# A hybrid decoder layer in float32 on one core: wide triples between bursts of chunk products, four array tiles at once, and 56 instead of 48 fill triples per group

## The chip, the core and the metric

The kernel runs on one core of one Trainium2 chip. The metric is device microseconds (us) of one execution; the figure compared is the median of several runs. The engines have short names here: PE is TensorE (matrix products; PEld its weight loads), DVE is VectorE, ACT is ScalarE, POOL is GpSimd, and SP is SyncE, which issues most DMAs.

## What is computed

One layer of a causal decoder, sequence 1024, width 1024, batch 1, all in float32. Cut to what matters:

```python
h = rms_norm(x, norm_mix_pre); z = h @ w_in          # ONE input projection for all branches and gates
z_pool, z_q, z_rwkv, z_gate = split(z)
y_pool = pool_branch(z_pool, ...) @ w_proj_pool
y_mem  = mem_attention(z_q, mem_n, w_mem_kv) @ w_proj_mem
zr = z_rwkv + (token_shift(z_rwkv) - z_rwkv) * mu_shift
r, k, v, dw, da, dg = split(zr)
def step(state, (rt, wt, kt, vt, an, bn)):           # 16 heads of 64, 1024 steps
    sa = state @ an
    state = state * wt + sa (x) bn + vt (x) kt       # (x): outer product
    yt = state @ rt
y_rwkv = (group_norm(y) + bonus) * g @ w_proj_rwkv
x = x + rms_norm((gates[0]*y_pool + gates[1]*y_rwkv + gates[2]*y_mem) @ w_o)
x = x + rms_norm((gelu(u_gate) * u_val) @ w_ffn_down)   # u = causal_dwconv(rms_norm(x) @ w_ffn_up)
```

The recurrence is done in 16 chunks of 64 steps: for each head and chunk a few 64x64 products, the inverse of a unit triangular 64x64 matrix, and then a short serial chain from chunk to chunk.

## The kernel before

**Wide triples.** A float32 product is made of three products of rounded parts: for a weight tile and 512 columns, `mm3` issues three matmuls of 128x128 by 128x512 (lines 180, 181, 182). I call these three a wide triple. Their weights come by DMA (`wraw`), are rounded on ACT (`whi`, line 132) and the rest is made on POOL (`wlo`, line 139).

**Preparations.** `rwkv_group(g, kv)` runs four times (g = 0 to 3), for four heads each, in two halves i = 0, 1 of 128 partitions (two heads, "lo" and "up"). In a group, in this order of the code:

- `lengths` (tile `phd`), then the decay and in-context rates (tile `psu`, lines 502 and 503), on ACT the sigmoids and exponentials, on DVE the scans and the factors `AR`, `BK`; the projection of r (`in_block(8 + p, ...)`, 48 wide matmuls per half) lies in between. The last reader of the scratch tile `tHV` is line 552.
- The centred values (tile `pv`, lines 577 and 578): 64 matmuls of 64x64 per group; each row of 64 partitions writes the other half of a PSUM tile. ACT copies them into `HV` (lines 579, 580), which has the memory of `tHV`.
- The chunk products (line 601): for each half i four bursts of 8 matmuls into two PSUM banks each; the four banks of `product_bank` (two of `pss`, one of `psk`, one of `psc`) go round, so a burst needs the banks of the burst before last. ACT copies two parts out of a burst (lines 605, 608) and DVE masks four (lines 606, 607, 609, 610).
- After the bursts of i = 0: the bonus (tile `pbo`, line 562, multiplied on DVE in line 563), and for each half the transposes of `BK` (tile `pt`, line 630, copied by ACT in line 631).
- The projection of the next group's k and v (`group_kv`, 192 wide matmuls), and on DVE the inverse of 32x32 blocks by 31 steps (lines 651 to 655), which ends with eight copies (line 664). Then PE joins the blocks: tile `pz` (line 672), copies by ACT and DVE, tile `pw` (line 680).

**Fill.** Blocks of the input projection that nobody needs soon (pool, query and gates: 32 blocks, 512 triples) are issued by `fill_to(n)`, which advances them until n triples are out. Before, a group asks for 48 more of them at the end of its solve; group 3 goes on to 256.

**Chain.** `chain` then walks over the 16 chunks with three visits each (tiles `pr`; `py` and `pu`; `ph` and `py`; all line 772). Before each visit it calls `fill_to(fills(visit))`: 262 at the first, then 279 rising to 400 at the last. Every two chunks use one set of loads (`ring`, `pair`, `hv`, `bk`, `rb`), sent ahead on SP's queue one per visit; the loads for chunks 2b and 2b+1 are sent during the two chunks before. Meanwhile the finished chunks are normed (tile `pvar`) and stored, and the fill's weights come on ACT's queue.

**Order.** A list scheduler orders the built instructions of each engine. `later(i, j)` is a dependence for that order alone; the engines wait for data and for buffers only.

Of the kernel before, what the change touches and what calls it, by code (L numbers as in the profile page):

```python
# [9 lines left out]
F32 = mybir.dt.float32  # L10
# [7 lines left out]
P = 128  # L18
# [3 lines left out]
C = 64  # L22
# [6 lines left out]
NF = 22  # L29
HK = NF // 2  # L30
LAST = HK - 4

PV = {}
_o = 0
# [10 lines left out]
def trunk_kernel(ctx: ExitStack, tc: tile.TileContext, xT, memT, pvec, w_in, w_kv, w_upd, w_upg,  # L45
                 w_pool, w_ppool, w_pmem, w_prwkv, w_o, w_fup, w_fdn, out):
    nc = tc.nc
    V, A, G, PE, SP = nc.vector, nc.scalar, nc.gpsimd, nc.tensor, nc.sync
# [53 lines left out]
    for lo in (0, 64):  # L102
        s = slice(lo, lo + 64)
# [371 lines left out]
    def rwkv_group(g, kv):  # L475
# [11 lines left out]
        def lengths():  # L487
            for i in range(2):
                for s, ps in square_sums(kv[i][:, 0], col("k_k", 2 * g + i), tHV[:, i, 1], sp[:, i]):
                    rstd(tHV[:, i, 1, s], ps, 1)  # L490

        if g:
            lengths()
            table(SIGMOID)
        for i in range(2):
            p = 2 * g + i
            uh, ul = load_up2(w_upd[p])
            for t0, _ in HALVES:
                s = slice(t0, t0 + 512)
                for e, l, dst, b in ((0, ld, tBN[i][:, 0, s], "w0"), (1, la, tHV[:, i, 0, s], "a0")):  # L500
                    ps = psg.tile([P, 512], F32, name="psu", tag="g0")
                    PE.matmul(ps, uh[:, e], l[:, s], start=True, stop=False)
                    PE.matmul(ps, ul[:, e], l[:, s], start=False, stop=True)
                    act(dst, ps, AF.Sigmoid, bias=col(b, p))
        table(LN_EXP)
        if g == 0:
            lengths()
        AR = rw.tile([P, 2, 3, T], F32, name="AR", tag="AR")
        vs = []
        turn = [0]  # L510

# [58 lines left out]
        NT = rw.tile([P, 2, NCH, C], F32, name="NT", tag="NT")  # L570
        HV = rw.tile([P, 2, NCH, C], F32, name="HV", tag="HV")
        for i in range(2):
            for c0 in (0, 8):
                ps = pss.tile([P, 8, C], F32, name="pv", tag="s")
                for c in range(8):
                    tsl = slice((c0 + c) * C, (c0 + c + 1) * C)
                    PE.matmul(ps[64:128, c], vs[i][0:64, tsl], cent[0:64], start=True, stop=True)
                    PE.matmul(ps[0:64, c], vs[i][64:128, tsl], cent[64:128], start=True, stop=True)
                A.copy(HV[64:128, i, c0:c0 + 8], ps[64:128])
                A.copy(HV[0:64, i, c0:c0 + 8], ps[0:64])  # L580
            spill(d_hv, (g, i), HV[:, i])


# [5 lines left out]
        for i in range(2):  # L589
            us = slice(NCH * i, NCH * i + NCH)  # L590
            for c0 in range(0, NCH, 4):
                def bc(m, q):
                    return m[q].unsqueeze(1).broadcast_to([64, 4, C])
                cs = slice(c0, c0 + 4)
                lo, up = slice(0, 64), slice(64, 128)
                ps = [product_bank("ps1"), product_bank("ps2")]
                m = None
                for c in range(4):
                    t = slice((c0 + c) * C, (c0 + c + 1) * C)
                    for e, rows in ((1, up), (0, lo)):  # L600
                        m, was = PE.matmul(ps[e][:, c], BK[i][rows, c0 + c], AR[rows, i, e:e + 2, t],
                                           start=True, stop=True), m
                        if was is not None:
                            later(m, was.ins)
                A.copy(RB[i][:, 0, cs], ps[0][:, :, 1])
                V.tensor_tensor(NT[lo, i, cs], ps[0][lo, :, 0], bc(mstrict, lo), op=ALU.mult)
                V.tensor_tensor(c3(AR[up, i, 0])[:, cs], ps[0][up, :, 0], bc(mstrict, up), op=ALU.mult)
                A.copy(RB[i][:, 1, cs], ps[1][:, :, 0])
                V.tensor_tensor(NT[up, i, cs], ps[1][up, :, 1], bc(mstrict, up), op=ALU.mult)
                V.tensor_tensor(c3(AR[lo, i, 2])[:, cs], ps[1][lo, :, 1], bc(mstrict, lo), op=ALU.mult)  # L610
            for e in range(2):
                V.tensor_tensor(RB[i][:, e], RB[i][:, e], mincl.unsqueeze(1).broadcast_to([P, NCH, C]),
                                op=ALU.mult)
# [13 lines left out]
            for c0 in range(0, NCH, 4):  # L627
                ps = pss.tile([P, 4, P], F32, name="pt", tag="s")
                for c in range(4):
                    PE.transpose(ps[:, c], BK[i][:, c0 + c], ident)  # L630
                A.copy(BKN[i][:, c0:c0 + 4], ps)
            SP.dma_start(d_bk[:, :, g, i].rearrange("c p u s -> p c (u s)"),
                         BKN[i].rearrange("p (c u) s -> p c (u s)", u=2))

            if i == 0:
                tb0 = rw.tile([P, 2, 32, 32], F32, name="tb0", tag=tagB[0])
            for q, (qs, bs) in enumerate(quads):
                if i == 0 or q < 2:
                    A.copy(tb0[qs, 1, us], NTu[qs, us, bs])
                else:  # L640
                    V.tensor_copy(tb0[qs, 1, us], NTu[qs, us, bs])
# [13 lines left out]
            V.tensor_tensor(S[:, s + 1:, 0:m], S[:, s + 1:, 0:m], tm, op=ALU.add)  # L655
        V.transpose(S11.rearrange("p u s -> p s u"), S.rearrange("p t s -> p s t"))
        V.transpose(X.rearrange("p u t -> p t u"), S)
        fill_to(48 * (g + 1))
        if g == 3:
            w_queue[0] = A  # L660
            fill_to(256, solve)
        for us in (slice(0, NCH), slice(NCH, 2 * NCH)):
            for q, (qs, bs) in enumerate(quads):
                place = V.tensor_copy(NTu[qs, us, bs], X[qs, us]).ins
        Z = tmp
        ends = [(slice(e, e + 32), slice(e + 32, e + 64)) for e in (0, 64)]
        for u0 in (0, 16):
            us = slice(u0, u0 + 16)
            ps = pss.tile([P, 16, 32], F32, name="pz", tag="s")
            for u in range(16):  # L670
                for q0, q1 in ends:
                    m = PE.matmul(ps[q1, u], NTu[q0, u0 + u, 32:64], S11[q0, u0 + u], start=True, stop=True)
                    if u0 == u == 0:
                        later(m, place)
            A.copy(Z[32:64, us], ps[32:64])
            V.tensor_copy(Z[96:128, us], ps[96:128])
            ps = pss.tile([P, 16, 32], F32, name="pw", tag="s")
            for u in range(16):
                for q0, q1 in ends:
                    PE.matmul(ps[q0, u], Z[q1, u0 + u], NTu[q1, u0 + u, 32:64], start=True, stop=True)  # L680
            for q0, q1 in ends:
                A.copy(NTu[q0, us, 32:64], ps[q0])


        for i in range(2):
# [161 lines left out]

    fill = [(j, spilled(d_zp[j])) for j in range(4)] + [(4 + j, spilled(d_zq[j])) for j in range(4)]
    fill += [(34 + j, spilled(d_zg[j], col("gate_b", j))) for j in range(24)]
    filled = []  # L850

    def fill_steps(j, evac, behind):

        ws = load_w(w_in[j], KC, c=1)
        for t0, _ in HALVES:
            ps = psg.tile([P, 512], F32, name="psg", tag="g1")
            rhs = hrhs(t0)
            for k in range(KC):
                m = mm3(ps, ws[k], rhs(k), k == 0, k == KC - 1)
                if k == 0 and behind is not None:  # L860
                    later(m, behind)
                filled.append(last_mm[0])
                if k == KC - 1:
                    evac(t0, ps)
                yield
# [3 lines left out]
    def fill_to(n, behind=None):  # L869

        while len(filled) < n:
            if next(current[0], 0) == 0:
                current[0] = fill_steps(*fill.pop(0), behind)
        return filled[n - 1]

    first_kv = start()
    for lo in (0, 64):
        s = slice(lo, lo + 64)
# [2 lines left out]
    hi_on_act[0] = True  # L881
    for g in range(4):
        kv = rwkv_group(g, kv)
    chain(lambda v: 279 + 121 * (v - 1) // 46 if v else 262)
    covered = fill_to(416)
    w_queue[0] = SP
    spare[0] = None
# [964 lines left out]
```

## Time and profile before

| | us |
|---|---|
| runs shown | 1952.37, 1947.69, 1952.64 (median 1952.37) |
| the profiled execution | 1947.9 |
| its span, first to last instruction | 1946.2 |
| first group's start to first `pr` of the chain | about 62 to 666 of the span |
| chain | 666 to 862 |
| attention, merge, feed-forward | 862 to the end |

In the profile, a row of the timeline has the start, the time from it to the end of the last of the xN merged instructions, engine, line, operation, tiles and form; in brackets stands the idle time of the engine before it and what ended that. A float32 matmul of a narrow kind is recorded as two instructions, so 8 of line 601 in the program are 16 records. A row of windows has the stretch, its length, the busy time and number of each engine's instructions, the granted PE clock as a share, the busy share of the 16 DMA engines and the GB/s.

### The profile page before, as it was taken

The page shows a single profiled execution, that of the slowest core. Times are in us where ns is not written, and L with a number is a line of the kernel's source. Part 1 is how long each engine was busy: PE and PEld are TensorE (multiplying, and loading weights), DVE is VectorE, ACT ScalarE, POOL GpSimd, SP SyncE. Part 2 cuts the span into 40 slices and gives each one's busy share as a digit, 9 for nine tenths or more (in the row PEclk, how much of TensorE's full clock was granted, in tenths as well). Part 3 has the DMA queues.
Part 4 walks back from the last instruction along what each step waited for, and adds up shares of the span by engine and source line. Part 5 has one row for each costly group of instructions (what it writes and reads, how often), then busy time and mean ns, then how long its engine had stood idle before and what let it go on. Part 6 is the DMA issues. An engine that isn't in the chain of part 4 may idle for free.

```text
span 1946.2 us, 33744 instructions
## 1 busy us (share of the span) xinstructions
PE 1886.9 (97%) x12204; PEld 1522.7 (78%) x12204; DVE 1356.7 (70%) x2022; ACT 1046.1 (54%) x2158; POOL 784.1 (40%) x867
## 2 busy tenths in 40 slices
PE   8999999999999999999999999999999999999997
PEld 6767777777777887778788888878788888888886
DVE  8677577677677345556964444679698888877798
ACT  7685385475474245455664344546554545454544
POOL 4422222222222211111323455556599889822441
PEclk9999999999999999999999999999999999999999
DMA  5326326335349669965336444653322222289775
GB/s 163 130 72 186 99 76 184 93 95 168 95 122 310 191 191 297 312 196 190 102 112 231 124 137 130 208 161 121 110 81 87 78 88 88 86 250 223 168 184 146
DMA packets 269639, 296.26 MB, mean 152 GB/s; under 512 B 18336, under 2 KB 219168, under 8 KB 266400
## 3 DMA queue, kind: packets, MB, share of 16 engines
q1 hardware_dynamic: 248480, 271.56, 44.8%
q0 software_dynamic: 11856, 14.16, 4.5%
q10 hardware_dynamic: 9136, 8.39, 1.4%
q8 instruction: 96, 1.57, 0.3%
q14 instruction: 71, 0.58, 0.1%
HBM read 207.00 MB, written 87.03 MB: 151 GB/s over the span
## 4 chain that ended last, share of the span: by engine, by line
PE 62%; DVE 5%; DMA 4%; issue 2%; ACT 2%; POOL 1%; ACTq 0%; POOLq 0%; DVEq 0%; SPq 0%
PE psg L180 10%; PE psg L182 10%; PE psg L181 10%; PE psf L182 6%; PE psf L180 6%; PE psf L181 6%; PE psd L181 2%; PE psd L182 2%; PE psd L180 2%; PE py L772 2%; PE pr L772 1%; DMA g<-d_zg 1%; PE ph L772 1%; PE pvar L716 1%; PE pu L772 1%
## 5 line engine op out<-in xcount | busy, mean ns | idle before, releaser
L139 POOL TENSOR_TENSOR wlo<-wraw,whi 128x256 fp32r<-128x256 f32 x464 | 403.0, 881 | 829.0 <-ACT whi L132 753.6
L180 PE MATMUL psg<-hh,whi 128*128 128x512 f32 x928 | 377.7, 407 | 12.4 <-ACT whi L132 9.0
L182 PE MATMUL psg<-hh,wlo 128*128 128x512 f32 x928 | 367.6, 397 | 1.8 <-POOL wlo L139 1.5
L181 PE MATMUL psg<-hl,whi 128*128 128x512 f32 x928 | 368.1, 397 | 0.7 <-DVE hl L266 0.6
L132 ACT CAST whi<-wraw 128x256 fp32r<-128x256 f32 x472 | 181.5, 403 | 246.8 <-PE psg L181 98.9
L180 PEld LDWEIGHTS psg<-hh,whi 128*128 128x128 f32 x928 | 174.8, 188 | 57.4 <-ACT whi L132 13.0
L182 PEld LDWEIGHTS psg<-hh,wlo 128*128 128x128 f32 x928 | 174.8, 188 | 44.1 <-POOL wlo L139 6.1
L181 PEld LDWEIGHTS psg<-hl,whi 128*128 128x128 f32 x928 | 175.0, 189 | 39.8 <-issue 4.3
L1178 POOL TENSOR_TENSOR wt<-a,wt 128x256 fp32r<-128x256 f32 x136 | 156.3, 1173 | 35.4 <-ACT wt L1177 35.2
L180 PE MATMUL psd<-f,u 128*128 128x512 f32 x292 | 113.3, 391 | 1.1 <-ACT f L1590 1.1
L181 PE MATMUL psd<-f,u 128*128 128x512 f32 x292 | 113.8, 390 | 0.5 <-DVE f L1594 0.5
L182 PE MATMUL psd<-f,u 128*128 128x512 f32 x292 | 113.6, 389 | 0.0
L182 PE MATMUL psf<-h2h,wt 128*128 128x512 f32 x272 | 105.9, 390 | 0.2 <-POOL wt L1178 0.2
L180 PE MATMUL psf<-h2h,wt 128*128 128x512 f32 x272 | 105.9, 389 | 0.1
L181 PE MATMUL psf<-h2l,wt 128*128 128x512 f32 x272 | 105.8, 389 | 0.0
L1192 DVE SCALAR_TENSOR_TENSOR d<-z,pv,d 128x1023 f32<-128x1023 f32 x68 | 101.1, 1491 | 2.2
L1178 POOL TENSOR_TENSOR wt<-s,wt 128x256 fp32r<-128x256 f32 x68 | 79.9, 1195 | 3.3 <-ACT wt L1177 2.0
L180 PE MATMUL psf<-t,wt 128*128 128x512 f32 x204 | 79.4, 389 | 0.0
L181 PE MATMUL psf<-t,wt 128*128 128x512 f32 x204 | 79.4, 389 | 0.0
L182 PE MATMUL psf<-t,wt 128*128 128x512 f32 x204 | 79.4, 389 | 0.0
L1190 ACT ACTIVATE d<-z,pv 128x1024 f32<-128x1024 f32 x34 | 42.4, 1248 | 65.8 <-DVE z L1272 50.1
L1177 ACT CAST wt<-a 128x256 fp32r<-128x256 f32 x136 | 50.7, 405 | 40.8 <-POOL wt L1178 28.1
(430 smaller groups left out, 4507.3 us busy)
## 6 DMA issues: line engine op xcount, KB each, us to landing
wraw<-in_w_in SPq DMA_DIRECT2D x176, 128.0 KB, 2.5
a<-in_w_fup SPq DMA_DIRECT2D x128, 128.0 KB, 2.4
d_ar<-AR SPq DMA_DIRECT2D x24, 512.0 KB, 4.2
d_zg<-st SPq DMA_DIRECT2D x48, 256.0 KB, 3.4
ring<-d_ar SPq DMA_DIRECT2D x8, 1536.0 KB, 10.8
wraw<-in_w_fup SPq DMA_DIRECT2D x80, 128.0 KB, 2.6
fraw<-d_f SPq DMA_DIRECT2D x33, 256.0 KB, 4.3
d_rb<-RB SPq DMA_DIRECT2D x16, 512.0 KB, 5.4
```

The source lines that it names most:

```text
L132: i = A.copy(hi, src)
L139: (V if lo_on_dve[0] else G).tensor_tensor(lo, src, hi.bitcast(F32), op=ALU.subtract)
L180: first = PE.matmul(ps, wh, xh, start=start, stop=False)
L181: PE.matmul(ps, wh, xl, start=False, stop=False)
L182: last_mm[0] = PE.matmul(ps, wl, xh, start=False, stop=stop).ins
L716: m = PE.matmul(ps, bones, q, start=True, stop=True)
L772: m = PE.matmul(out_, l, r, **kw)
L1177: A.copy(w[0][:, us], src[u])
L1178: low = eng.tensor_tensor(w[1][:, us], src[u], w[0][:, us].bitcast(F32), op=ALU.subtract)
L1190: A.activation(d, z, AF.Identity, scale=col("cw2", j), bias=col("cb", j))
L1192: V.scalar_tensor_tensor(d[:, n:], z[:, :T - n], col(cw, j), d[:, n:], op0=ALU.mult, op1=ALU.add)
```

## The change

It has five parts. (1) Between two bursts of chunk products stand two wide triples of the fill. (2) `pv`, `pz` and `pw` are issued so that four array tiles (two row groups by two column groups) follow each other; all copies of `pz` precede all of `pw`. (3) A group asks for 56 triples instead of 48, group 3 goes to 288 instead of 256, and the chain starts from there: 294 at its first visit, then 311 rising to 400. (4) At the head of groups 1 to 3 two lots of six triples are asked for behind fixed places, and one triple in group 0. (5) Two half tiles of `pv` (i = 1) use the banks `psk` and `psc` instead of `pss`.

```diff
+GROUP = 56
+TAKEN = 4 * GROUP + 64
...
+        cover, burst = [GROUP * g - 12 if g else 0], [None]
+
+        def covered(n, behind=None):
+            cover[0] += n
+            fence[0] = behind
+            wide = fill_to(cover[0])
+            fence[0] = None
+            return wide
+
+        if g:
+            covered(6, placed[0])
+            covered(6, raised[2])
+        else:
+            covered(1)
...
-            for c0 in (0, 8):
-                ps = pss.tile([P, 8, C], F32, name="pv", tag="s")
-                for c in range(8):
-                    tsl = slice((c0 + c) * C, (c0 + c + 1) * C)
-                    PE.matmul(ps[64:128, c], vs[i][0:64, tsl], cent[0:64], start=True, stop=True)
-                    PE.matmul(ps[0:64, c], vs[i][64:128, tsl], cent[64:128], start=True, stop=True)
+            ps = [pool.tile([P, 8, C], F32, name="pv", tag=tag)
+                  for pool, tag in (((psk, "k"), (psc, "c")) if i else ((pss, "s"), (pss, "s")))]
+            m = None
+            for c in range(8):
+                for n in (1, 0):
+                    t = slice((8 * n + c) * C, (8 * n + c + 1) * C)
+                    for rows, at_ in ((lo, lo if n else up), (up, up if n else lo)):
+                        m, was = PE.matmul(ps[n][at_, c], vs[i][rows, t], cent[rows], start=True, stop=True), m
+                        later(m, was.ins if was is not None else raised[-1])
...
                 ps = [product_bank("ps1"), product_bank("ps2")]
-                m = None
+                after = covered(2, burst[0]) if c0 else None
...
-        fill_to(48 * (g + 1))
+        fill_to(GROUP * (g + 1) - (12 if g < 3 else 0))
         if g == 3:
             w_queue[0] = A
-            fill_to(256, solve)
+            fill_to(TAKEN, solve)
...
-        for u0 in (0, 16):
-            us = slice(u0, u0 + 16)
-            ps = pss.tile([P, 16, 32], F32, name="pz", tag="s")
+        us = slice(0, 16), slice(16, 32)
+        ps = pss.tile([P, 16, 32], F32, name="pz", tag="s")
+        for u in range(16):
+            for h in range(2):
+                for ends_ in ends:
+                    m = PE.matmul(ps[ends_[1 - h], u], NTu[ends_[0], 16 * h + u, 32:64],
+                                  S11[ends_[0], 16 * h + u], start=True, stop=True)
...
-    chain(lambda v: 279 + 121 * (v - 1) // 46 if v else 262)
+    chain(lambda v: TAKEN + 23 + (377 - TAKEN) * (v - 1) // 46 if v else TAKEN + 6)
```

How this stands in the built order of PE, at the three places that the prediction rests on. (The new file has other line numbers: 601 became 623, 562 became 579, 630 became 654, 772 became 804, and 180 to 182 became 182 to 184.) First, the bursts of chunk products of group 3, i = 0, where the second burst (tiles `ps_5514`/`ps_5515`) ends; before:

```order
L601 MATMUL ps_5515<-AR,BK_5131 128x128
L601 MATMUL ps_5514<-AR,BK_5131 128x128
L181 MATMUL psg<-hl,whi 128x512
L601 MATMUL ps_5531<-AR,BK_5131 128x128
L601 MATMUL ps_5530<-AR,BK_5131 128x128
```

and now, where the first burst (`ps_5624`/`ps_5625`) ends:

```order
L623 MATMUL ps_5625<-AR,BK_5190 128x128
L623 MATMUL ps_5624<-AR,BK_5190 128x128
L182 MATMUL psg<-hh,whi 128x512
L183 MATMUL psg<-hl,whi 128x512
L184 MATMUL psg<-hh,wlo 128x512
L182 MATMUL psg<-hh,whi 128x512
L183 MATMUL psg<-hl,whi 128x512
L184 MATMUL psg<-hh,wlo 128x512
L623 MATMUL ps_5641<-AR,BK_5190 128x128
L623 MATMUL ps_5640<-AR,BK_5190 128x128
```

One wide matmul after two bursts became six after each of the first three; all eight sets of bursts look like this now.

Second, PE behind the last burst of i = 0 in group 3, with the bonus (`pbo`); before, wide matmuls stand between its parts, and two, sixteen and two more between the transposes that follow:

```order
L601 MATMUL ps_5546<-AR,BK_5131 128x128
L182 MATMUL psg<-hh,wlo 128x512
L562 MATMUL pbo<-kv_4343,bonesr 128x512
L180 MATMUL psg<-hh,whi 128x512
L181 MATMUL psg<-hl,whi 128x512
L182 MATMUL psg<-hh,wlo 128x512
L180 MATMUL psg<-hh,whi 128x512
L562 MATMUL pbo<-kv_4343,bonesr 128x512
```

and now, down to the first burst of i = 1:

```order
L623 MATMUL ps_5685<-AR,BK_5190 128x128
L579 MATMUL pbo<-kv_4484,bonesr 128x512 x2
L579 MATMUL pbo<-kv_4647,bonesr 128x512 x2
L654 MATMUL pt<-ident,BK_5190 128x128 x16
L623 MATMUL ps_5777<-AR,BK_5191 128x128
```

No wide matmul is left there in group 3; groups 0 to 2 keep theirs (35 instead of 37 or so).

Third, PE in the chain, from `pr` to `py` of chunk 8; before three triples, now two:

```order
L772 MATMUL pr<-hv,ring 64x64 x16
L180 MATMUL psg<-hh,whi 128x512
L181 MATMUL psg<-hl,whi 128x512
L182 MATMUL psg<-hh,wlo 128x512
L180 MATMUL psg<-hh,whi 128x512
L181 MATMUL psg<-hl,whi 128x512
L182 MATMUL psg<-hh,wlo 128x512
L180 MATMUL psg<-hh,whi 128x512
L181 MATMUL psg<-hl,whi 128x512
L182 MATMUL psg<-hh,wlo 128x512
L772 MATMUL py<-ring,hv 64x64 x16
```

```order
L804 MATMUL pr<-hv,ring 64x64 x16
L182 MATMUL psg<-hh,whi 128x512
L183 MATMUL psg<-hl,whi 128x512
L184 MATMUL psg<-hh,wlo 128x512
L182 MATMUL psg<-hh,whi 128x512
L183 MATMUL psg<-hl,whi 128x512
L184 MATMUL psg<-hh,wlo 128x512
L804 MATMUL py<-ring,hv 64x64 x16
```

The sixteen triples that two chunks held here became twelve; nothing else in the chain's order of PE moved.

More of the change, by code (lines that the diff above doesn't have):

```diff
@@ L490, in lengths @@
                     rstd(tHV[:, i, 1, s], ps, 1)
+        raised = []
         if g:
@@ L502, in rwkv_group @@
                     PE.matmul(ps, uh[:, e], l[:, s], start=True, stop=False)
-                    PE.matmul(ps, ul[:, e], l[:, s], start=False, stop=True)
+                    raised.append(PE.matmul(ps, ul[:, e], l[:, s], start=False, stop=True).ins)
                     act(dst, ps, AF.Sigmoid, bias=col(b, p))
@@ L572, in rwkv_group @@
         for i in range(2):
-            for c0 in (0, 8):
-                ps = pss.tile([P, 8, C], F32, name="pv", tag="s")
-                for c in range(8):
-                    tsl = slice((c0 + c) * C, (c0 + c + 1) * C)
[L577 to L580, printed above, removed]
+            lo, up = slice(0, 64), slice(64, 128)
+            ps = [pool.tile([P, 8, C], F32, name="pv", tag=tag)
[7 more added lines that the diff above has]
+                        later(m, was.ins if was is not None else raised[-1])
+            for n in range(2):
+                A.copy(HV[up, i, 8 * n:8 * n + 8], ps[n][lo if n else up])
+                A.copy(HV[lo, i, 8 * n:8 * n + 8], ps[n][up if n else lo])
             spill(d_hv, (g, i), HV[:, i])
@@ L600, in rwkv_group @@
                     for e, rows in ((1, up), (0, lo)):
[L601 to L604, printed above, removed]
+                        m = PE.matmul(ps[e][:, c], BK[i][rows, c0 + c], AR[rows, i, e:e + 2, t],
+                                      start=True, stop=True)
+                        if after is not None:
+                            later(m, after)
+                        after = m.ins
+                burst[0] = after
                 A.copy(RB[i][:, 0, cs], ps[0][:, :, 1])
@@ L664, in rwkv_group @@
                 place = V.tensor_copy(NTu[qs, us, bs], X[qs, us]).ins
+        placed[0] = place
         Z = tmp
         ends = [(slice(e, e + 32), slice(e + 32, e + 64)) for e in (0, 64)]
-        for u0 in (0, 16):
-            us = slice(u0, u0 + 16)
-            ps = pss.tile([P, 16, 32], F32, name="pz", tag="s")
[L670 to L673, printed above, removed]
-                        later(m, place)
[L675 to L682, printed above, removed]
+        us = slice(0, 16), slice(16, 32)
[5 more added lines that the diff above has]
+                                  S11[ends_[0], 16 * h + u], start=True, stop=True)
+                    if u == h == 0:
+                        later(m, place)
+        for h in range(2):
+            moved = [A.copy(Z[32:64, us[h]], ps[ends[0][1 - h]]),
+                     V.tensor_copy(Z[96:128, us[h]], ps[ends[1][1 - h]])]
+        ps = pss.tile([P, 16, 32], F32, name="pw", tag="s")
+        for u in range(16):
+            for h in range(2):
+                for ends_ in ends:
+                    m = PE.matmul(ps[ends_[h], u], Z[ends_[1], 16 * h + u],
+                                  NTu[ends_[1], 16 * h + u, 32:64], start=True, stop=True)
+                    for i in moved:
+                        later(m, i.ins)
+        for h in range(2):
+            for ends_ in ends:
+                A.copy(NTu[ends_[0], us[h], 32:64], ps[ends_[h]])
         for i in range(2):
@@ L849, in trunk_kernel @@
     fill += [(34 + j, spilled(d_zg[j], col("gate_b", j))) for j in range(24)]
-    filled = []
+    filled, fence = [], [None]
     def fill_steps(j, evac, behind):
@@ L861, in fill_steps @@
                     later(m, behind)
+                if fence[0] is not None:
+                    later(m, fence[0])
                 filled.append(last_mm[0])
@@ L874, in fill_to @@
         return filled[n - 1]
+    placed = [None]
     first_kv = start()
```

## The prediction

> **What bounds the kernel now.** I read the page, then the busy times by stage, then the idle time by line, then the timeline of one set of bursts.
>
> ```profile
> PE 1886.9 (97%) x12204; PEld 1522.7 (78%) x12204; DVE 1356.7 (70%) x2022; ACT 1046.1 (54%) x2158; POOL 784.1 (40%) x867
> 62.00:666.00 604.00, 577.20 (x4183) 454.44 (x4183) 417.01 (x701) 363.98 (x689) 151.83 (x176) 0.98 0.46 139
> 666.00:862.00 196.00, 195.99 (x2938) 155.70 (x2938) 90.75 (x128) 95.67 (x239) 29.30 (x36) 1.00 0.82 254
> 610.00:650.00 40.00, 40.00 (x178) 33.13 (x177) 0.00 (x0) 4.80 (x7) 1.00 0.79 273
> L601 PE MATMUL ps<-AR,BK 64*128 64x128 f32 x512 | 42.1, 319 | 15.2 <-DVE AR L610 8.0 <-ACT RB L605 7.1
> ```
>
> PE carries the program. Of 604 us of preparations it sits 26.8 us idle, and 15.2 of these are in front of the chunk products; in the chain it never idles. The third windows row holds wide matmuls alone: 40 us over 178, two of them cut by the edges, so one costs 0.227 us and a triple 0.68. Work moved from one place to another where PE is full costs nothing; only what fills or opens idle PE time counts, and what makes PE work itself cheaper.
>
> **The bursts.** In group 3, i = 0:
>
> ```profile
> 569.46 2.08 PE L601 MATMUL ps<-AR,BK 64*128 64x128 f32 x32
> 571.47 0.51 PE L181 MATMUL psg<-hl,whi 128*128 128x512 f32 x1
> 573.38 1.16 PE L601 MATMUL ps<-AR,BK 64*128 64x128 f32 x16 [1.41 <-DVE AR L610]
> 575.14 1.16 PE L601 MATMUL ps<-AR,BK 64*128 64x128 f32 x16 [0.60 <-DVE AR L610]
> 577.07 1.10 PE L562 MATMUL pbo<-kv,bonesr 128*128 128x512 f32 x2 [0.33 <-DVE AR L610]
> 578.29 0.42 DVE L610 TENSOR_TENSOR AR<-ps,mstrict 64x256 f32<-64x256 f32 x1
> 807.80 0.40 PE L182 MATMUL psg<-hh,wlo 128*128 128x512 f32 x1
> 808.13 1.15 PE L772 MATMUL py<-ring,hv 64*64 64x64 f32 x32
> 810.14 0.50 PE L180 MATMUL psg<-hh,whi 128*128 128x512 f32 x1
> 810.48 0.39 PE L181 MATMUL psg<-hl,whi 128*128 128x512 f32 x1
> 453.30:456.70 3.40, 3.40 (x32) 3.32 (x31) 2.60 (x7) 2.24 (x8) 0.73 (x1) 0.50 0.00 0
> sum 67.20, PE 42.11 PEld 37.45; mean PE 5.26 PEld 4.68
> ```
>
> Two bursts run in 2.01 us (1.0 each), then PE waits until DVE frees banks. DVE needs four masks of 0.43, 1.75 us a burst. The chain's rows price a change of shape: 807.80 to 808.13 is 0.33 (0.10 over a wide matmul), 810.14 to 810.48 is 0.34 (0.11). The row at 453.30 shows a second price: right after such a wait the granted clock is 0.50 for 3.4 us. There are five such stretches, four of them inside the eight sets of bursts and one mostly, each worth up to 1.7 us of work. The last row sums the windows of all eight sets, first chunk product to the next other work: 67.2 us, with 25 wide matmuls in them by the order.
>
> New: four bursts of 1.0 and three covers of 6 x 0.227 + 0.24 = 1.6 make 8.8 us a set, 70.4 in all, holding 144 wide matmuls. DVE's 1.75 us fits under a burst and its cover (2.6), so I cost the waits at nothing; if DVE were late, each cover would end in a wait as now. Gain: 67.2 - 70.4 + 119 x 0.227 = **23.8 us**.
>
> **Four tiles at once.**
>
> ```profile
> 566.93 0.22 PE L577 MATMUL pv<-cent,kv 64*64 64x64 f32 x1
> 566.93 0.22 PE L578 MATMUL pv<-cent,kv 64*64 64x64 f32 x1
> 566.99 0.22 PE L577 MATMUL pv<-cent,kv 64*64 64x64 f32 x1
> 515.18 1.20 PE L672 MATMUL pz<-tb,NT 32*32 32x32 f32 x64
> 516.31 0.50 PE L502 MATMUL psu<-ld,uhi 128*128 128x512 f32 x1
> ```
>
> Today two tiles start together and the next pair 0.058 us later; 128 records of `pv` a group cost 4 us, `pz` and `pw` 64 in 1.13 us, twice each, 4.5. With four tiles a step the bounds are no gain (the pair's step) and half. I take half, since a pair starts within 0.01 us and four starts fit into 0.058: 2 us a group for `pv`, 2.2 for `pz` and `pw`.
>
> The Trainium skill, page "TensorEngine Tiling (Array Packing)", Restrictions and Gotchas (Gotcha 1), states that different row tiles cannot access the same PSUM bank simultaneously. New `pv` writes a bank from both row groups, so by that rule nothing overlaps across rows, and the sum would be that of the first rival. Today's pairs also write one bank from two row groups and start together; this trace does not bear the rule out.
>
> But less PE work is worth something only where PE is the bound. At the head of groups 1 to 3, from `pz` to the first chunk product:
>
> ```profile
> 230.01:282.78 52.77, 37.67 (x152) 27.80 (x151) 3.11 (x6) 3.87 (x6) 1.00 0.26 75
> 371.65:424.14 52.49, 37.67 (x152) 27.79 (x151) 3.11 (x6) 3.87 (x6) 1.00 0.28 79
> 515.18:569.46 54.28, 38.18 (x155) 28.36 (x154) 3.10 (x6) 4.80 (x7) 1.00 0.33 97
> 524.20 1.17 ACT L682 COPY NT<-pw 32x512 f32<-32x512 f32 x2 [2.69 <-PE pw L680]
> 563.75 1.76 DVE L552 SCALAR_TENSOR_TENSOR kv<-AR,pv,tHV 128x1024 f32<-128x1024 f32 x1
> 565.54 0.58 ACT L579 COPY HV<-pv 64x512 f32<-64x512 f32 x1 [1.22 <-DVE kv L552]
> ```
>
> `HV` lies on `tHV`, so `pv` can't leave PSUM before line 552 of i = 1 is done: now 50.3 us after `pz` in group 3. That chain (ACT's copies of `pw`, roots, sigmoids, exponentials, then DVE without a pause) starts 2 us earlier when `pw` is earlier by 3.2 and ACT has two more copies (1.17) ahead. I estimate line 552 at 45 us after `pz` (43 to 48), the last needed bank (`psk`, after six ACT copies of 0.58) at 48.6. PE's own work to there falls to some 42, so PE idles about 4 us, and the half clock may follow. Three heads: 159.5 us with 459 wide matmuls become 145.8 with 410 (program counts, up to the first full burst): 13.7 - 49 x 0.227 = **2.6 us** gained, less 1.5 for the clock. Group 0 has no such head in front; `pv` gains **1.9** there, and `pz` and `pw` before the chain **1.9** (2.2 less a later store of `NT`, two ACT copies behind).
>
> **The uncovered bonus of group 3.** PE has only `pbo` and `pt` from the last burst of i = 0 to i = 1:
>
> ```profile
> 577.07:591.53 14.46, 9.59 (x34) 6.17 (x34) 0.00 (x0) 0.69 (x1) 1.00 0.88 262
> 578.63 2.34 DVE L612 TENSOR_TENSOR RB<-RB,mincl 128x1024 f32<-128x1024 f32 x2
> 583.99 0.69 DVE L563 TENSOR_TENSOR kv<-kv,pbo 128x512 f32<-128x512 f32 x1 [0.17 <-PE pbo L562]
> 584.72 1.15 ACT L564 ACTIVATE kv<-kv,pv 128x1024 f32<-128x1024 f32 x1 [1.18 <-DVE kv L563]
> 589.35 1.07 ACT L631 COPY BKN<-pt 128x512 f32<-128x512 f32 x2 [1.81 <-DMA d_bv<-kv]
> ```
>
> Now 14.46 us hold 34 wide matmuls, 7.7 us. New: masks 1.9 after the last burst, line 612 to 4.2, multiplications to 7.1, line 564 to 8.3, three ACT copies of `pt` to 10.2, then the bank is free: 10.4 us. Cost 10.4 + 7.7 - 14.5 = 3.6, and 0.9 for half clock after it: **-4.5** (-3 to -7).
>
> **The chain.** 32 triples leave it (262 asked at the start becomes 294, the end stays 400), 21.8 us shorter if PE stays the bound; as moved work this counts nothing. What is new is what may come up behind it:
>
> ```profile
> 744.90:841.00 96.10, 96.10 (x1486) 75.86 (x1485) 49.74 (x72) 50.64 (x129) 12.41 (x16) 1.00 0.97 305
> wraw<-in_w_in ACTq DMA_DIRECT2D x20, 128.0 KB, 6.2
> d_zg<-st SPq DMA_DIRECT2D x10, 256.0 KB, 4.5
> rb<-d_rb SPq DMA_DIRECT2D x5, 1024.0 KB, 5.9
> 810.40 0.68 DVE L809 COPY hv<-pu 64x512 f32<-64x512 f32 x1
> 811.35 0.58 ACT L810 COPY hv<-pu 64x512 f32<-64x512 f32 x1
> ```
>
> PE and the DMA engines are both full: 24.2 us for two chunks (96.1 over four pairs), DMA share 0.97. Four triples fewer a pair make 21.5 us of PE work. They take 65 KB each off the DMA (20 x 128 and 10 x 256 KB over 80 triples), 0.26 of 7.4 MB, so DMA needs 24.2 x 0.97 x 0.965 = 22.6: 1.1 us late per pair, five pairs 5.5. `rb` is sent one chunk (10.8) before its use and lands after 5.9, a reserve of some 4.5, which takes most of it. The copies behind `pu` end 1.8 us after it (DVE, then ACT); two triples and `pvar` cover 2.5, one triple and `pvar` 1.7. I take **-3.5** (0 to -14).
>
> **Sum.** 23.8 + 2.6 - 1.5 + 1.9 + 1.9 - 4.5 - 3.5 = 20.7 us off the profiled execution's 1947.9: 1927. That execution is 4.5 under the median of 1952.37; the runs lie at two levels (1947.7 and 1952.5), so I go half way up: **1929 us**. What can be told from no change is about 0.3%, 6 us.
>
> **Rivals.**
>
> *Row tiles don't share the array.* For it: no row shows four tiles; against: the pairs. `pv` gains nothing, the heads start 2.2 us later, the chain's start 2.2: 20.7 - 1.9 - 2.2 - 6.6, gain 10: 1939. Chance 0.13.
>
> *The DMA engines hold the chain.* The pairs stay at 24.2 us, five times 2.7 lost instead of 3.5: gain 10, 1939. For it: share 0.97; against: a reserve per load. The Trainium skill, page "Trainium Kernel Development and Optimization", Key Constraints, states that queues of SP, ACT and POOL run on the same 16 DMA engines; by that, weights on ACT's queue are no way round, and the shares above agree. Chance 0.10.
>
> *The covers wait for their weights: slower.*
>
> ```profile
> 182.22 0.50 PE L180 MATMUL psg<-hh,whi 128*128 128x512 f32 x1 [1.17 <-ACT whi L132]
> ```
>
> A cover is one `whi` of two triples, and its cast stands in ACT's order behind the burst's copies. If each of 24 covers waits as here, 1.2 us, 28 us go, and 1957 results; it decides from 20.7 / 24 = 0.9 us a cover. Against: weights serve two halves of a block, and buffers hold a block. Chance 0.07.
>
> *More than forecast.* The bonus of group 3 and the chain cost nothing, the heads run at full clock: 1929 - 9.5 = 1919. Chance 0.10.
>
> **How the numbers follow.** The forecast has 0.60, its own range 1920 to 1936. With both rivals of 1939 and part of the better one the range is 1914 to 1943, leaving out the slow rival and the tails. Faster by over 0.3% (under 1946): nearly all of the forecast and of the better case, most of the two at 1939: 0.88. Same 0.06, slower 0.06.
>
> **What would show it.** Line 601's idle falls from 15.2 to under 4 and no window of 3.4 us at clock 0.50 stays in the bursts. `pz` takes 0.6 us for 64 records, not 1.13. First chunk product 46 to 49 us after `pz`. Group 3 shows 10 us from the last burst of i = 0 to i = 1 with PE idle. The chain takes 174 to 178 us instead of 196 with DMA share near 1.0. I am wrong if PE waits for `whi` in the covers, if the chain stays over 185 us, or if a head takes over 50.

## The result and the profile after

The changed kernel takes 1966.11 us (median of 6 runs, 1962.82 to 1971.27), the kernel before 1948.46 (6 runs beside it): ratio 1.0087, interval 1.0071 to 1.0104. It is slower by 17 us; the forecast was 1929. Its profiled execution took 1965.81 us, with a span of 1964.1.

The idle time by line, PE only. The change moved the line numbers: 623 is the old 601 (chunk products), 654 the old 630, 579 the old 562, 598 the old 577 and 578, 505 the old 502. The second fence has the same line of `psu` in the kernel before:

```profile
L623 PE MATMUL ps<-AR,BK 64*128 64x128 f32 x512 | 41.0, 295 | 11.4 <-ACT HV L602 11.3
L654 PE MATMUL pt<-ident,BK 128*128 128x128 f32 x128 | 19.5, 288 | 10.2 <-ACT BKN L655 8.3 <-DVE AR L634 1.1 <-ACT RB L632 0.5
L579 PE MATMUL pbo<-kv,bonesr 128*128 128x512 f32 x32 | 16.5, 618 | 4.3 <-DVE AR L634 2.6 <-DVE kv L580 1.7
L505 PE MATMUL psu<-ld,uhi 128*128 128x512 f32 x16 | 9.6, 600 | 12.8 <-ACT tBN L216 12.8
```

```profile
L502 PE MATMUL psu<-ld,uhi 128*128 128x512 f32 x16 | 6.7, 417 | 0.0
```

The waits of the chunk products for masks (DVE 8.0, ACT `RB` 7.1) are gone: the covers do what they say. In their place the chunk products wait 11.3 us for ACT's copies of `HV`, `psu` waits 12.8 us where it waited for nothing, and `pt` 10.2 instead of 0.9. The `psu` wait is the one that I had not thought of. PE at the head of group 1:

```profile
239.23 0.50 PE L473 MATMUL phd<-sp,bonesr 128*128 128x512 f32 x1 [0.38 <-ACT tHV L216]
239.57 0.40 PE L474 MATMUL phd<-sp,bonesr 128*128 128x512 f32 x1
244.24 0.79 PE L505 MATMUL psu<-ld,uhi 128*128 128x512 f32 x1 [4.28 <-ACT tBN L216]
244.83 0.63 PE L506 MATMUL psu<-ld,ulo 128*128 128x512 f32 x1
243.80:250.60 6.80, 6.36 (x14) 4.22 (x15) 3.69 (x4) 4.40 (x7) 1.69 (x2) 0.50 0.10 32
```

The last row is a stretch of the windows view: 6.8 us at a granted clock of 0.50. `psu` has two PSUM buffers (tag `g0`). The third product must wait until ACT has taken the first by its sigmoid, and ACT does that only behind all the roots of `phd` and a table load. In the kernel before wide matmuls and `pv` stood in that place; now the first six triples stand ahead of it and the next six behind the third `psu`, so nothing can run. The end of the same head, ACT, DVE and PE together:

```profile
277.85 2.09 PE L598 MATMUL pv<-cent,kv 64*64 64x64 f32 x128
278.09 0.68 ACT L331 ACTIVATE AR<-psg,omu 128x512 f32<-128x512 f32 x1
278.80 0.22 DVE L335 SCALAR_TENSOR_TENSOR AR<-zc,pv,AR 128x1 f32<-128x1 f32 x1 [4.75 <-ACT AR L331]
279.72 1.28 DVE L569 SCALAR_TENSOR_TENSOR kv<-AR,pv,tHV 128x1024 f32<-128x1024 f32 x1
281.09 0.58 ACT L601 COPY HV<-pv 64x512 f32<-64x512 f32 x1 [2.32 <-DVE kv L569]
281.68 0.58 ACT L602 COPY HV<-pv 64x512 f32<-64x512 f32 x1
282.31 0.48 PE L623 MATMUL ps<-AR,BK 64*128 64x128 f32 x2 [2.37 <-ACT HV L602]
```

DVE stood idle 4.75 us for ACT, and ACT for PE: line 569 needs `r`, whose last projection matmul stands right in front of `pv` (277.85). PE itself sets the length of the head, through `r`; and since all twelve triples stand ahead of `r`, only `pv` is left to run while DVE and ACT finish. The heads, wide matmuls alone (the fourth row is group 3 from the last burst of i = 0 to i = 1, the last the chain):

```profile
228.67:282.31 53.64, 32.66 (x133) 24.83 (x132) 3.12 (x6) 3.89 (x6) 0.94 0.25 72
379.84:434.55 54.71, 32.39 (x133) 24.76 (x132) 3.12 (x6) 3.89 (x6) 0.94 0.26 76
532.12:584.73 52.61, 32.17 (x133) 24.47 (x132) 3.12 (x6) 4.11 (x6) 0.97 0.28 84
598.43:613.77 15.34, 0.00 (x0) 0.00 (x0) 0.00 (x0) 0.00 (x0) 0.85 0.85 249
707.24:881.79 174.55, 174.29 (x2840) 137.50 (x2840) 85.98 (x128) 91.01 (x227) 21.65 (x28) 1.00 0.86 276
```

The heads are about as long as before (52.8, 52.5, 54.3) and hold 132 wide matmuls instead of 151 to 154. Group 3's stretch holds none, where 34 stood. The chain is 21.1 us shorter, as forecast, without a stall.

To add stages up I take from each stage's length its wide matmuls at 0.2275 us (the same 2496 in all kernels of the table, so their place costs nothing). What is left, in us of the profiled spans:

| stage | before | changed | covers_only | psu_four_buffers | psu4_all |
|---|---|---|---|---|---|
| head of group 0 | 30.5 | 33.5 | 34.8 | 33.7 | 32.3 |
| heads of groups 1 to 3 | 55.8 | 70.9 | 87.9 | 53.2 | 44.2 |
| eight sets of bursts | 56.8 | 48.3 | 40.8 | 51.9 | 45.9 |
| bonus and transposes behind i = 0 | 29.0 | 39.5 | 35.2 | 39.9 | 31.6 |
| i = 1's last burst to `pz` | 14.6 | 15.9 | 15.7 | 16.4 | 16.9 |
| last `pz` to the chain | 5.7 | 3.6 | 5.7 | 3.4 | 3.2 |
| chain | 101.5 | 102.2 | 102.9 | 101.9 | 101.9 |
| behind the chain | 1084.5 | 1082.3 | 1080.2 | 1083.4 | 1080.0 |

The heads lose 15.1 and the bonus 10.5 (8.0 of it in group 3); the bursts win only 8.4.

### The profile page after: what moved, and what is told of

The parts are those of the page before. It is cut to its first block, busy times and chain, and to the rows that moved or that the text cites. A ratio compares the mean times of both kernels' runs of the same rounds, so it can differ in the third digit from the quotient of the medians.

```text
span 1964.1 us, 33713 instructions
## 1 busy us (share of the span) xinstructions
PE 1882.8 (96%) x12204; PEld 1511.3 (77%) x12204; DVE 1346.3 (69%) x2022; ACT 1047.3 (53%) x2158; POOL 777.1 (40%) x867
## 3 DMA queue, kind: packets, MB, share of 16 engines
q8 instruction: 96, 1.57, 0.3%
## 4 chain that ended last, share of the span: by engine, by line
PE 61%; DMA 4%; DVE 3%; issue 2%; ACT 1%; POOL 1%; SPq 0%; POOLq 0%; ACTq 0%; DVEq 0%
PE psg L182 11%; PE psg L184 10%; PE psg L183 10%; PE psf L184 5%; PE psf L182 5%; PE psf L183 5%; PE psd L183 2%; PE psd L184 2%; PE psd L182 2%; PE py L804 2%; DMA Q<-in_w_fdn 1%; PE pr L804 1%; PE ph L804 1%; PE pu L804 1%; DMA R<-d_f 1%
## 5 line engine op out<-in xcount | busy, mean ns | idle before, releaser
L141 POOL TENSOR_TENSOR wlo<-wraw,whi 128x256 fp32r<-128x256 f32 x464 | 395.0, 863 | 892.7 <-ACT whi L134 786.3
```

The source lines that it names most:

```text
L141: (V if lo_on_dve[0] else G).tensor_tensor(lo, src, hi.bitcast(F32), op=ALU.subtract)
```

## The experiments

All ratios are against the kernel before, run beside them; its median was 1948.5 us beside the changed kernel and 1950.1 to 1950.7 beside the experiments. Theory H came from the trace after: the covers are drawn from one stream of triples, which goes in order through two banks, so a triple that is fenced to a late place holds back all behind it; the places that this stream had covered, behind `phd`, behind `r` and in the bonus of group 3, lie bare.

**The parts alone.**

```diff
 # covers_only, on the kernel before
+                after = covered(2, burst[0]) if c0 else None
 # four_tiles_only, on the kernel before: the new pv, pz, pw; in pv, against the changed kernel:
-                        later(m, was.ins if was is not None else raised[-1])
+                        if was is not None:
+                            later(m, was.ins)
 # g56_only, on the kernel before
-        fill_to(48 * (g + 1))
+        fill_to(56 * (g + 1))
-            fill_to(256, solve)
+            fill_to(288, solve)
```

> The kernel before with one part of the change: two triples between bursts, 48 triples per group and 256 before the chain as before, old inverse and values. Theory H (the heads of groups 1 to 3 lost their cover): the 36 wide matmuls of the covers come out of the heads, where PE now has pw, phd, psu and the projection with nothing between; the eight sets gain about 17 us, three heads lose some 8 us each, so about 1955 us (1950 to 1962), with PE idle by some 5 us behind phd and some 4 us between the last wide matmul and the first chunk product. Rival P (covers gain what was forecast and the loss of the whole change comes from the reordered values or from the 56 triples): 1925 to 1932 us.

> The kernel before with the new inverse and values alone (four tiles at once), without covers, without the place behind the last psu, 48 triples per group. By the sum of the prediction: values of group 0 1.9, inverse before the chain 1.9, heads at most 2 each. Theory H adds that values now stand ahead of psu and nothing stands behind r any more, so that the heads give nothing (0 +- 2 each): about 1946 us (1941 to 1951). Rival F (the four-tile order itself costs, by more copies on ACT ahead of the roots): 1952 to 1957 us.

> The kernel before with 56 triples per group and 288 before the chain, nothing else. Theory H: where PE is full a moved triple costs nothing: groups longer by 5.5 us each and 5.5 more ahead of the chain for 21.8 us less in the chain and behind it, about 1950 us (1946 to 1953). Rival L (the shorter chain waits for its loads, as the rival of the DMA engines has it): chain no shorter than 185 us, 1955 to 1962 us.

Measured: covers_only 1975.51 us (1.0138, 1.0122 to 1.0155), four_tiles_only 1950.21 (1.0007, 0.9990 to 1.0024), g56_only 1951.8 (1.0002, 0.9988 to 1.0017). The covers carry the loss; the two other parts alone are worth nothing that can be told. Theory H had the sign of covers_only and 20 us too little: its sets gain 16.0, but its heads lose 32 (the table). four_tiles_only came out in H's range, 1941 to 1951, but at its upper end. The wide matmuls of its heads of groups 1 and 3, and what waits behind `phd` in group 1:

```profile
231.38:285.54 54.16, 27.69 (x117) 21.40 (x116) 3.09 (x6) 3.31 (x5) 0.94 0.25 71
524.30:578.56 54.26, 22.52 (x97) 17.85 (x96) 3.10 (x6) 3.41 (x5) 0.87 0.29 85
244.54 0.27 PE L586 MATMUL pv<-cent,kv 64*64 64x64 f32 x1 [0.54 <-ACT tHV L214]
248.16 0.51 PE L502 MATMUL psu<-ld,uhi 128*128 128x512 f32 x1 [1.53 <-ACT tBN L214]
```

116 and in group 3 only 96 (the projection `r` and nothing else) where 151 to 154 stood; the head does not get shorter for it. That g56_only comes out even shows that 32 triples can go from chain to groups for nothing, as the forecast said.

**What the heads lack.**

```diff
 # behind_r, on the changed kernel: the second six triples
-            covered(6, raised[2])
...
             in_block(8 + p, shifted(p, r_))
+            if g and i:
+                covered(6, last_mm[0])
 # before_psu, on the changed kernel: the same six
+            hole = covered(6, phd_last[0])
...
+                    if g and len(raised) == 2:
+                        later(m, hole)
 # both_covers: before_psu and behind_r, six each, six fewer under the solve
```

> The changed kernel, but the second six triples of a head stand behind the last matmul of its projection r instead of behind the third psu. Theory H: r ends 4.1 us earlier in each head, so DVE's last two operations and ACT's copies of HV run under the six triples, and the first chunk product comes 4 us earlier: 3 x 4 = 12 us, about 1954 us (1950 to 1958). Rival S (only the hole behind phd, where psu waits for its two buffers, is the loss, and what stands behind it makes no difference): 1963 to 1967 us.

> The changed kernel, but the second six triples of a head stand between the last phd and the third psu. Theory H and rival S agree on the place: the wait of 4.3 us in front of psu falls under 1 us, the half clock behind it goes, r ends 4 to 6 us earlier and with it the first chunk product: 3 x 5 = 15 us, about 1951 us (1947 to 1956). Rival D (a head is set by ACT and DVE behind pw, whatever PE does): 1963 to 1967 us.

> The changed kernel with six triples between the last phd and the third psu and six more behind the last matmul of r, taken from the stretch under the solve, where DVE is done about 7 us before pz. Theory H: the heads are as long as in before_psu and hold 18 more wide matmuls each, 3 x 4.1 = 12 us more: about 1939 us (1934 to 1945), faster than the kernel before. Rival S: no better than before_psu, about 1951 us, since the six triples behind r only displace others.

Measured: 1959.55 us (1.0044, 1.0032 to 1.0056), 1959.29 (1.0044, 1.0032 to 1.0056) and 1950.39 (0.9996, 0.9987 to 1.0006). Each place gives 7 us against the changed kernel, half of what H expected, so rival D falls, and rival S of behind_r. Both together give 15.7: both_covers is 9 us faster than before_psu, against rival S, but H's 1939 was missed by 11 us, and 1950.4 is no faster than the kernel before. In before_psu the wait went from 12.8 to 1.3:

```profile
L518 PE MATMUL psu<-ld,uhi 128*128 128x512 f32 x16 | 7.2, 450 | 1.3 <-ACT tBN L216 1.3
```

The first chunk product came 2.7 to 4.5 us earlier in a head, not 5, for PE then waits longer for `HV`: 19.0 us in front of the chunk products, where the changed kernel has 11.3. The chain lost 2.9 us in waits, mostly for `rb` and `hv`.

**Group 3's bonus.**

```diff
 # g3_cover, on the changed kernel, in group 3 and i = 0
+        lots = list((2, 3, 0, 0, 1, 5, 0, 0)) if g == 3 else []
...
-                PE.matmul(ps, bones, t0_[:, s], start=True, stop=True)
+                between(PE.matmul(ps, bones, t0_[:, s], start=True, stop=True))
 # between(m) puts the next lot of triples behind m; the transposes have it too
 # all_covers: both_covers and g3_cover
```

> The changed kernel, with eleven of group 3's triples put by hand between the products of its bonus and the transposes of i = 0 (2, 3, 1 and 5 triples, each lot behind one of them), in the places where groups 1 and 2 have wide matmuls; as many fewer stand under the solve. Theory H (the fenced covers of i = 1 hold back every later triple, so this stretch of group 3 runs with no wide matmul): the stretch stays at 15 to 16 us and now holds 33 wide matmuls, 7.5 us, and the half clock in front of i = 1 goes, 0.9: about 8 us less than the changed kernel, 1957.5 us (1955 to 1960). Rival M (the stretch is held by its DMA loads or by PE itself, so that the triples lengthen it): 1963 to 1967 us.

> both_covers and g3_cover in one. Theory H: the two losses are in different places and add up: 1950.4 - 8 = about 1942 us (1939 to 1946), faster than the kernel before by 0.4%. Rival M: 1948 to 1951 us.

Measured: 1962.04 us (1.0056, 1.0038 to 1.0075) and 1940.12 (0.9954, 0.9942 to 0.9966). Alone the median fell by 4 us, half of what H expected and just below rival M's range; on top of both_covers it fell by 10.3. PE in this stretch, first of the changed kernel, then the windows view of all_covers with wide matmuls alone:

```profile
598.43 1.13 PE L579 MATMUL pbo<-kv,bonesr 128*128 128x512 f32 x2
601.07 1.10 PE L579 MATMUL pbo<-kv,bonesr 128*128 128x512 f32 x2 [1.51 <-DVE AR L634]
603.84 1.98 PE L579 MATMUL pbo<-kv,bonesr 128*128 128x512 f32 x4 [1.68 <-DVE kv L580]
611.88 1.97 PE L654 MATMUL pt<-ident,BK 128*128 128x128 f32 x8 [4.61 <-ACT BKN L655]
613.77 2.08 PE L623 MATMUL ps<-AR,BK 64*128 64x128 f32 x16
```

```profile
582.50:597.50 15.00, 8.34 (x33) 5.82 (x33) 0.00 (x0) 1.37 (x2) 1.00 0.96 290
```

The stretch is 15 us long with or without 33 wide matmuls, so the 7.5 us were bare waiting; with a DMA share of 0.96 it did not grow, and rival M falls. In g3_cover's own trace the stretch falls as expected (15.5 to 8.0 by the reckoning of the table), but the bursts take 2.3 us longer and the stretches ahead of `pz` 1.0, so that 4.0 of the span are left; why these grow stays open (the interval of its runs is 7 us wide).

**What four tiles and 56 triples are worth then.**

```diff
 # copies_split, on all_covers
+                copy = V.tensor_copy if g and i and not n else A.copy
...
 # all_covers_pairs: pv, pz and pw of the kernel before
 # all_covers_48
-GROUP = 56
+GROUP = 48
```

> all_covers with DVE making two of the eight copies of HV (i = 1, the half in psk) in groups 1 to 3. Theory H: what is left of the heads' loss is PE's wait of 1.5 to 2 us for ACT's sixth copy of HV in front of the first chunk product and the half clock behind it; the bank is free 1.1 us earlier, the half clock goes in part: 3 x 2 = 6 us, about 1934 us (1931 to 1938). Rival D (DVE's two copies push its last operation AR, which the chunk product needs too, so nothing is won): 1939 to 1942 us.

> all_covers with the old inverse and values (two tiles at once). It prices the four tiles where PE is covered. Theory H: values 2 us and inverse 2.2 us a group come back, of the inverse 1.9 ahead of the chain too: about 12 us slower than all_covers, 1952 us (1946 to 1956). Rival F (four tiles are worth nothing here, as in four_tiles_only): 1938 to 1943 us.

> all_covers with 48 triples per group and 256 before the chain. Theory H: the covers now take 18 of a group's triples from the stretch under the solve; DVE had some 3 us to spare there at 56, so with eight triples (5.5 us) fewer pz waits about 2.5 us for DVE in groups 1 to 3: 3 x 2.5 = 7 us slower than all_covers, about 1947 us (1943 to 1951). Rival N (the number of triples per group is neutral, as in g56_only): 1938 to 1942 us.

Measured: copies_split 1939.76 us (0.9948, 0.9936 to 0.9960), all_covers_pairs 1952.21 (1.0006, 0.9997 to 1.0015), all_covers_48 1946.07 (0.9972, 0.9960 to 0.9984). By the medians the four tiles are worth 12 us where PE is covered and nothing where it isn't; eight triples more a group are worth 6 us, where the covers draw on them. For these H had the size and only a part of the cause: in the trace of all_covers_48 `pz` waits for DVE once, 2.17 us in group 0, not in groups 1 to 3, and the half clock behind that wait (6.8 us from 228.78) goes with a head of 57.7 us, 5.7 longer than in all_covers. copies_split gave nothing: my reading was wrong. The row at 282.31 above shows the first chunk product released by the second copy, 1.3 us behind line 569, not by the sixth; in all_covers it is the third. The rest of that burst does wait for a later copy, but six wide matmuls stand in between; in all_covers PE waits there in group 3 alone, 1.91 us.

**`psu`'s buffers.**

```diff
 # psu_four_buffers, on the changed kernel
-                    ps = psg.tile([P, 512], F32, name="psu", tag="g0")
+                    pool, tag = ((psg, "g0"), (psg, "g0"), (psk, "k"), (psc, "c"))[len(raised) % 4] if g else (psg, "g0")
+                    ps = pool.tile([P, 512], F32, name="psu", tag=tag)
 # before_psu4: the same on the kernel before; covers_psu4: on covers_only
 # psu4_g3: on g3_cover; psu4_all: psu4_g3 and six triples behind r from under the solve
```

> The changed kernel with four PSUM buffers for psu in groups 1 to 3 (its two, and the banks psk and psc, which are free there), nothing moved by hand. Theory H: psu's two buffers make the hole; with four, the third and fourth psu run ahead of pw and the covers fenced behind the third fill the time behind phd: the wait of 4.3 us goes, as in before_psu, about 1959 us (1956 to 1962). Rival T (the hole is ACT's own time for roots, table and sigmoids, so PE waits as long with four buffers, one psu later): 1964 to 1968 us.

> The kernel before with four PSUM buffers for psu in groups 1 to 3, nothing else. Theory H: psu waits there 0.2 to 0.3 us a head, since wide matmuls stand between its pairs; four buffers give nothing, 1950.5 us (1947 to 1953). Rival G (the buffers speed up any such kernel, and so are no cause of the change's loss): 1935 to 1943 us.

> covers_only with four PSUM buffers for psu. Theory H: here 36 wide matmuls are gone from each head, and no triple is there that could run behind phd, so the wait stays, only earlier sigmoids are won: 1966 to 1975 us. Rival B (the buffers are the whole loss of the covers too): 1954 to 1961 us, as much less as psu_four_buffers.

> psu_four_buffers with group 3's eleven triples between the products of the bonus (as g3_cover). Theory H: two separate losses, 1951.3 - 8 = about 1943 us (1941 to 1947): the whole of the change's loss and some 7 us of gain. Rival: 1949 to 1952 us, if the two overlap.

> psu4_g3 with six triples more behind the last matmul of r in each head, taken from the stretch under the solve (as both_covers has them). Theory H: they fill the wait of some 4 us for ACT's copies of HV, 3 x 3 = 9 us less than psu4_g3, about 1934 us (1930 to 1939). Rival U (DVE under the solve has no time to spare, or the heads grow by as much): 1941 to 1946 us.

Measured: psu_four_buffers 1951.28 us (1.0008, 0.9994 to 1.0021), before_psu4 1948.88 (0.9996, 0.9982 to 1.0009), covers_psu4 1968.77 (1.0091, 1.0065 to 1.0116), psu4_g3 1943.75 (0.9968, 0.9952 to 0.9983), psu4_all 1929.32 (0.9897, 0.9877 to 0.9918). One of the six executions of covers_psu4 took 5169 us; the ratio leaves it out, and the median of the other five is 1966.73.

Two more buffers, and nothing moved by hand, take the changed kernel back to the time of before: 15 of its 17 us. The kernel before gains nothing from them, so they are no general gain. In covers_only they win 7 to 9 of 25; H's reason is that no triple is left there that could run behind `phd`. In psu_four_buffers the third and fourth `psu` run ahead of `pw`, as H had it, and the second six triples run behind `phd`. Its line of `psu`, its heads, and PE at the end of the first head:

```profile
L506 PE MATMUL psu<-ld,uhi 128*128 128x512 f32 x16 | 7.3, 457 | 0.9 <-ACT tBN L216 0.9
229.00:277.36 48.36, 32.35 (x133) 24.24 (x132) 3.11 (x6) 3.90 (x6) 1.00 0.27 80
377.72:425.19 47.47, 32.80 (x136) 24.96 (x135) 3.09 (x6) 3.91 (x6) 1.00 0.29 85
521.57:569.69 48.12, 32.40 (x133) 24.25 (x132) 3.11 (x6) 4.10 (x6) 0.99 0.30 92
277.36 0.49 PE L624 MATMUL ps<-AR,BK 64*128 64x128 f32 x2 [4.15 <-ACT HV L603]
```

With the hole closed (0.9 us of waits instead of 12.8) the heads are 48 us, within the 46 to 49 that the prediction gave, the clock is 1.00, and the next wait stands where H put it: 4.15 us for `HV`. Six triples behind `r` cover it in psu4_all:

```profile
223.54:272.88 49.34, 36.25 (x151) 27.77 (x150) 3.10 (x6) 4.48 (x7) 1.00 0.27 78
366.15:413.99 47.84, 36.23 (x151) 27.75 (x150) 3.10 (x6) 4.49 (x7) 1.00 0.28 83
506.38:555.75 49.37, 36.21 (x151) 27.77 (x150) 3.10 (x6) 4.78 (x7) 1.00 0.32 93
272.88 0.49 PE L633 MATMUL ps<-AR,BK 64*128 64x128 f32 x2 [0.91 <-ACT HV L612]
```

The heads hold as many wide matmuls as in the kernel before and are 3 to 5 us shorter. psu4_all beats both kernels, by 1.0% and 1.9%. H missed in two places. It expected psu_four_buffers no better than before_psu, and it is 8 us better. By the traces 3.5 of these are in the chain (177.8 and 174.3 us), 4.9 between `pz` of group 1 and `pz` of group 2; why was not traced further. And psu4_all is 14 us faster than psu4_g3, where H expected 9: 8.9 of them are in the heads by the reckoning of the table (53.1 and 44.2), the rest mostly in the bursts and in the head of group 0.

## Why the prediction was wrong, step by step

Terms of the sum against the table, changed less before:

| step | forecast | measured |
|---|---|---|
| bursts | -23.8 | -8.4 (-16.0 in covers_only) |
| heads of groups 1 to 3, with half clock | -1.1 | +15.1 |
| bonus and transposes behind i = 0 | +4.5 | +10.5 |
| head of group 0 | -1.9 | +3.0 |
| `pz` and `pw` before the chain | -1.9 | -2.1 |
| chain | +3.5 | +0.7 |
| i = 1's last burst to `pz`, and behind the chain | 0 | -0.9 |
| sum | -20.7 | +17.9 |

**The step that failed is the heads**, and it is a step of reasoning, not of size. The prediction let the chain start at ACT's copies of `pw` and run "without a pause" to line 552 at 45 us after `pz`. In group 1 it ended 52.3 us after it (279.72 + 1.28 - 228.67), because it needs `r`, and `r` came from a PE that had waited: 4.3 us at `psu`, then up to 6.8 us at half clock. I counted PE's work in the head (some 42 us, 4 idle) and not its order: which instruction stands behind `phd` when ACT is late, and how many `psu` fit into two buffers. The order of the changed kernel showed eight matmuls of `psu` behind `phd` with no wide matmul among them, where the old one has `pv` and wide matmuls; the two buffers were in the code. psu_four_buffers removes this one thing and the heads come out at 48 us, which settles it as the main cause of the loss against the kernel before. It does not bring the forecast: the kernel is then where it was before, and the other missed terms, below, hold back the 20.7 us of gain.

**The bursts** were right in mechanism: no wait for masks or `whi` remains in the covers, and the half clock of these waits is gone in the i = 1 sets of groups 0 to 2 (9.0 us, against 8.8 forecast). The size was off twice. Of 23.8 us, covers_only has 16.0. The forecast's windows ran to the next other work and counted the wait behind the last burst of a set as removed, and that wait stays, in front of `pbo` and `pt`; this is 4.7 of the missing 7.8 (67.2 - 25 x 0.227 = 61.5, where the table has 56.8). The rest is in the sets themselves, of which the last takes 10.5 us instead of 8.8. Another 7.6 went in the changed kernel, all of it in i = 0, behind the first products, which wait for `HV`: 3.4 us at clock 0.50 in group 2 and 6.8 in group 3, and in group 3 a second wait of 1.91 for `HV`. One reading of the prediction was off as well: of its five stretches at half clock, the one from 429.39 lasts 6.8 us, not 3.4.

**Group 3's bonus** was seen, but it lasts 15.3 us, not 10.4. ACT's rows there:

```profile
606.59 1.15 ACT L581 ACTIVATE kv<-kv,pv 128x1024 f32<-128x1024 f32 x1 [1.02 <-DVE kv L580]
611.24 1.07 ACT L655 COPY BKN<-pt 128x512 f32<-128x512 f32 x2 [3.50 <-DMA d_bv<-kv]
```

Line 581 (the old 564) ends 9.3 us into the stretch, 1.0 later than forecast. Then ACT waits 3.5 us for the store of the bonus, since `BKN` lies on `kv`. The prediction quoted the same wait (1.81 us) from the trace before, and let the copies follow at once.

**Group 0** had no gain from `pv` but a loss of 3.0. The row below is the largest new wait in its head; why ACT's cast is later there was not tried.

```profile
117.32 0.50 PE L182 MATMUL psg<-hh,whi 128*128 128x512 f32 x1 [1.59 <-ACT whi L134]
```

**Four tiles at once** run as taken: 128 records of `pz` in 1.22 us up to the next product (the row below runs to the end of the last record), of `pv` in 2.09. Alone, in four_tiles_only, they were worth nothing that can be told; the 2.1 us ahead of the chain did come.

```profile
228.67 1.29 PE L697 MATMUL pz<-tb,NT 32*32 32x32 f32 x128
```

The rule of the Trainium skill that row tiles cannot access one bank together (page "TensorEngine Tiling (Array Packing)", Restrictions and Gotchas, Gotcha 1) does not hold in these rows: `pv` writes each bank from both row groups and took 4 us a group before. In the trace the two records of a `pbo` of 512 columns start 0.43 us apart, so a record of 64 columns needs some 0.054 us by itself, and four records of `pv`, two into each of two banks, start in every 0.058 us. **The chain** was right: 174.55 us in the forecast's 174 to 178, with 0.2 us of waits for loads. **The rivals**: the two of 1939 fall, the row tiles by the 2.09 us of `pv`, the DMA engines by the chain. Covers that wait for `whi` named the right sign for a wrong reason: no record of the covers waits in the traces of the changed kernel and of covers_only, and PE waits in other places. The prediction's own condition, a head of over 50 us, is what came true.

## What to carry to other kernels

Filler work is a single stream in order: to put it into one gap is to take it out of others, so before moving it, list every place that it covers today, and what each would wait for without it. Where PE looks full, read the order behind each producer whose consumer is another engine, and count the PSUM buffers: two buffers in a row of eight products stop PE as soon as the reader is late. Work that must feed another engine at the end of a stage (`r` here) goes ahead of the filler, and the filler behind it.

## What the runs showed of the hardware

The half clock does not follow from the length of the wait alone. In all_covers and in copies_split PE waits 2.01 and 2.04 us in front of the same product; 1.2 to 1.3 us later a wide matmul takes 0.63 in the first and 0.40 in the second:

```profile
276.01 0.49 PE L635 MATMUL ps<-AR,BK 64*128 64x128 f32 x2 [2.01 <-ACT HV L614]
277.33 0.63 PE L182 MATMUL psg<-hh,whi 128*128 128x512 f32 x1
```

```profile
276.51 0.48 PE L636 MATMUL ps<-AR,BK 64*128 64x128 f32 x2 [2.04 <-ACT HV L615]
277.73 0.40 PE L182 MATMUL psg<-hh,whi 128*128 128x512 f32 x1
```

The traces show a difference between the two. In all eighteen of them the granted clock changes only on a raster of 3.41 us, which lies differently in each trace, and up to the end of the chain a stretch at 0.50 lasts one, two or three whole steps of it (3.41, 6.83 or 10.24 us). In all_covers the whole wait falls into one step, and the next step is at 0.50. In copies_split the raster cuts the wait into 1.3 and 0.8 us, and no step is at 0.50. The windows of two steps each, first of all_covers, then of copies_split:

```profile
273.69:277.10 3.41, 1.40 (x28) 1.05 (x18) 1.65 (x2) 2.83 (x5) 0.00 (x0) 1.00 0.27 77
277.10:280.51 3.41, 3.41 (x19) 2.56 (x17) 0.00 (x0) 2.70 (x7) 0.00 (x0) 0.50 1.03 292
```

```profile
272.33:275.75 3.42, 2.15 (x122) 1.84 (x120) 3.35 (x4) 1.62 (x3) 0.28 (x1) 1.00 0.26 77
275.75:279.16 3.41, 2.65 (x18) 1.99 (x20) 1.50 (x3) 2.51 (x6) 0.00 (x0) 1.00 0.71 194
```

How much idle time within a step is enough does not come out of the traces: in the kernel before, the step from 425.97 has 1.57 us idle and half clock follows; in behind_r the step from 427.83 has 2.00 us idle, and none follows. That the place of a wait on the raster decides is thus argued from these rows; no run tried it by moving a wait alone. A wait of this length may therefore cost up to 1.7 us more, or nothing, from one kernel to the next, and perhaps from one execution to the next.
